# Conv blocks 1 to 3 stay in SBUF and their layernorm is held in code order; two more scheduling conditions

## The chip, the cores and the metric

One core of one Trainium2 chip. The time is device microseconds (us) of one execution, the median of three runs: 2671.15 before the change (2670.78 to 2677.89).

## What is computed

One encoder layer over 2048 tokens of width 1024 in float32, with 256 memory tokens (`rmsnorm`, `layernorm` and the projections are the usual ones):

```python
y = rmsnorm(h, norm_mix_g) @ w_in                      # q, k, v of 8 heads; a, g of the conv branch
att = dilated_sliding_attention(q, k, v)               # windows 128, 512, 2048 at dilations 1, 4, 16
u = a * sigmoid(g)
u = depthwise_conv(u, width 31, 512 channels) + conv_b
conv = silu(layernorm(u, conv_ln_g, conv_ln_b))        # mean and variance over the 512 channels
h = h + concatenate([att, conv]) @ w_out
h = h + cross_attention(rmsnorm(h), rmsnorm(mem)) @ w_xo
h = h + square(relu(rmsnorm(h) @ w_up)) @ w_down
return rmsnorm(h, norm_final_g)
```

The three dilated attentions of a head are joined by a softmax over their log-denominators.

## The kernel before

Tokens are split into four blocks of 512 (p = 0 to 3). Activations lie transposed, channels on the 128 partitions and 512 tokens along a row, so the 512 conv channels are four tiles of 128x512 (c = 0 to 3). Matrix products are done as three fp16 matmuls (`mm3`, L374 to L376), of high and low halves; `split_to` makes the two halves of a weight tile, the high one on ACT (L361) and the low one on DVE (L362).

For each block, `post(p)` does the out projection (`o`, weights `ws_o`), cross attention (`x`, `s`), and the MLP (`up`, `dn`). While `post(p)` runs, the attention of block p+1 and the convolution of block p+1 are woven into it as side generators; for p = 1 and 2 the weight combinations of the MLP (`pw`, `ps`, `pt`) are a third side. The convolution of "pass n" (block n) therefore runs inside `post(n-1)`: its layernorm lies near 1000 to 1090 us for pass 1, 1580 to 1660 for pass 2, 2110 to 2200 for pass 3. Pass 0's is part of the first stage and its layernorm runs beside the first attention.

- `conv_unit` (L391): for each c, 31 multiply-adds on DVE from `cu` into `cacc`, and a store of `cacc` to DRAM (`cscr`).
- `conv_ln` (L411 to L456): loads the four tiles back as `lc`; sums them on DVE (L414, L415, L416); column sums by PE against ones (`lps..m`, L411); a broadcast back by PE (`lrb`, L355), subtraction (L424), squares on ACT (L425, L427), `lps..v`, a Newton rsqrt on DVE (L348 to L350), a second broadcast (`lrc`), the product on DVE (L439, four of them); silu on ACT (L442, four, ahead of them a table load), and the split of the result into `lhl` (ACT L450, DVE L451), stored to `cath` and `catl`.
- `combine` (L1164 to L1202): joins the three attentions of a head pair; L1164 is its first step on DVE, a minimum over `ld`, which a DMA loads from `oscr`.
- In the MLP of blocks 1 and 2, `quad` forms products by a scheme with seven or eight block products, named B11, T1, T32, T4 and so on; its copies (ACT L1656), sums (DVE L1660), relu (L1662), squares (ACT L1664) and splits (L1632, L1633) free PSUM for the next product.
- `norm` in `post` (L1801 ff.): the rms sum of the MLP's input, PE `nps` (L1468), DVE rsqrt, PE `nrb` (L355), ACT copy into `rsb`. For p < 2 it runs in two steps, one behind each of the first two up tiles.

The order on each engine is decided by a scheduler that simulates a timeline. The code influences it by `after(stack, names)`: instructions issued inside may not be put ahead of the last instruction noted under these names ("pe", "dve", "act": `last[...]`, noted at some lines). `pinned(gen, names)` does that for every step of a generator. Pools give each tag a number of buffers.

Of the kernel before, what the change touches and what calls it, by code (L numbers as in the profile page):

```python
# [10 lines left out]
F32 = mybir.dt.float32  # L11
# [4 lines left out]
AF = mybir.ActivationFunctionType  # L16
ALU = mybir.AluOpType
# [4 lines left out]
P = 128  # L22
# [26 lines left out]
def hybrid_layer(ctx, tc, A, out):  # L49
# [7 lines left out]
    def dma(o, i, q=None):  # L57
        return (q or nc.sync).dma_start(o, i)
# [18 lines left out]
    last = {}  # L77
# [6 lines left out]
    def pinned(gen, *names):  # L84

        while True:
            with ExitStack() as st:
                after(st, *names)
                if next(gen, st) is st:
                    return  # L90
            yield
# [267 lines left out]

    def split_to(t, raw, scale):  # L360
        ACT.activation(t[:, 0], raw, AF.Copy, scale=scale)  # L361
        DVE.scalar_tensor_tensor(t[:, 1], raw, scale, t[:, 0], op0=ALU.mult, op1=ALU.subtract)  # L362
        return t

    def two(t):
# [18 lines left out]
        dma(u, uscr[c][:, 512 * n:512 * n + 542])  # L384
        return u

    def conv_unit(c, n, alloc, u):
        acc = alloc("acc", (P, 512), f"cacc{c}_{n}")
        DVE.tensor_scalar(acc, u[:, 0:512], cw[:, c, 0:1], gain("conv_b", c), op0=ALU.mult, op1=ALU.add)
        for t in range(1, CW):  # L390
            DVE.scalar_tensor_tensor(acc, u[:, t:t + 512], cw[:, c, t:t + 1], acc, op0=ALU.mult, op1=ALU.add)  # L391
            if t % 4 == 0:
                yield
        dma(cscr[c][:, 512 * n:512 * (n + 1)], acc)
        yield

    def conv_ln(n, alloc):
        sl = slice(512 * n, 512 * (n + 1))
        cs = []
        for c in range(4):  # L400
            t = alloc(f"cs{c}", F32, f"lc{n}_{c}")
            dma(t, cscr[c][:, sl])
            cs.append(t)
# [520 lines left out]
    def ln_tiles(pl):  # L924
        def alloc(role, dtype, name, shape=(P, 512)):
            if role[:3] == "col":
                return pl.tile(list(shape), F32, tag="cl_" + role, name=name)
            if role[:2] == "cs":
                return pl.tile(list(shape), F32, tag="u" if role[2] < "2" else "acc", name=name, bufs=2)
            return pl.tile(list(shape), dtype, tag="vr", name=name, bufs=2)  # L930
        return alloc

    def conv_units(pl, n, cs=(0, 1, 2, 3), ahead=True):
        def alloc(role, shape, name):
            return pl.tile(list(shape), F32, tag=role, name=name, bufs=2)

        u = conv_load(cs[0], n, alloc)
        yield
        yield
        for i, c in enumerate(cs):  # L940
            nxt = conv_load(cs[i + 1], n, alloc) if ahead and i + 1 < len(cs) else None
            yield from conv_unit(c, n, alloc, u)
            u = nxt or (conv_load(cs[i + 1], n, alloc) if i + 1 < len(cs) else None)

    def conv(pl, n):

        yield from pinned(conv_units(pl, n), "dve")
        yield from conv_ln(n, ln_tiles(pl))

    def both(*gens):  # L950
        for _ in zip(*gens):
# [193 lines left out]
    def combine(p, pr, o0):  # L1145
# [14 lines left out]
        mm_ = sm_[:, 0].rearrange("p (j h) -> p j h", h=2)  # L1160
        W = DVE if end or p > 1 else POOL
        with ExitStack() as st:
            after(st, "dve")
            DVE.tensor_tensor(mm_, ld[:, 0, :, :, HD + 1], ld[:, 1, :, :, HD + 1], op=ALU.min)  # L1164
            DVE.tensor_tensor(mm_, mm_, o0[:, :, :, HD + 1], op=ALU.min)
        W.tensor_tensor(e3[:, 0], mm_, o0[:, :, :, HD + 1], op=ALU.subtract)
# [526 lines left out]
    def post(p):  # L1693
# [104 lines left out]

        def norm(step, st={}):

            if step == 0:  # L1801
                st[0] = rstd_from(ssum)
            elif step == 1:
                rb = ps("c", "nrb")
                bcast_rows(rb, st[0], 4)
                ACT.activation(rsb, rb, AF.Copy, scale=K_UP)

        held = None if p > 1 else []
        if held is None:
# [344 lines left out]
```

## Time and profile before

| what | value |
|---|---|
| runs | 2677.89, 2670.78, 2671.15 us |
| profiled execution | 2675.08 us |
| its span, first to last instruction | 2673.3 us |
| mean granted TensorE clock | 0.993 |
| PE, DVE, ACT, POOL busy | 97%, 73%, 46%, 8% |

Times in the profile count from the span's start. A timeline row has the start, the duration, the engine and line, the operation with its output and inputs, a count, and in brackets the idle time ahead of it on that engine and what ended it.

### The profile page before, as it was taken

The page shows a single profiled execution, that of the slowest core. Times are in us where ns is not written, and L with a number is a line of the kernel's source. Part 1 is how long each engine was busy: PE and PEld are TensorE (multiplying, and loading weights), DVE is VectorE, ACT ScalarE, POOL GpSimd, SP SyncE. Part 2 cuts the span into 40 slices and gives each one's busy share as a digit, 9 for nine tenths or more (in the row PEclk, how much of TensorE's full clock was granted, in tenths as well). Part 3 has the DMA queues.
Part 4 walks back from the last instruction along what each step waited for, and adds up shares of the span by engine and source line. Part 5 has one row for each costly group of instructions (what it writes and reads, how often), then busy time and mean ns, then how long its engine had stood idle before and what let it go on. Part 6 is the DMA issues. An engine that isn't in the chain of part 4 may idle for free. (4 is left out here: it accounts for less than half of the span.)

```text
span 2673.3 us, 45710 instructions
## 1 busy us (share of the span) xinstructions
PE 2602.2 (97%) x17782; PEld 1660.2 (62%) x17782; DVE 1942.8 (73%) x3751; ACT 1236.1 (46%) x2182; POOL 226.4 (8%) x285
## 2 busy tenths in 40 slices
PE   8999999999899999999999999999999999999998
PEld 7844448766454455445576676555776674468876
DVE  5886656577679996556699985467999856676566
ACT  5737545476455344434553343255443434453223
POOL 1234102132002011000000000000000000000000
PEclk9999999999999999999999999999999999999999
DMA  9977968665626777865357677454787775345442
GB/s 268 296 258 219 285 225 264 184 193 170 171 84 172 232 223 213 269 189 171 105 164 221 217 226 232 143 169 123 221 267 242 243 245 159 100 136 163 156 139 80
DMA packets 447048, 523.66 MB, mean 196 GB/s; under 512 B 89997, under 2 KB 341825, under 8 KB 446064
## 3 DMA queue, kind: packets, MB, share of 16 engines
q1 hardware_dynamic: 439424, 505.73, 61.8%
q10 hardware_dynamic: 5184, 9.01, 0.9%
q0 software_dynamic: 2224, 6.01, 0.6%
q8 instruction: 139, 2.28, 0.4%
q14 instruction: 77, 0.63, 0.1%
HBM read 389.18 MB, written 131.48 MB: 195 GB/s over the span
## 5 line engine op out<-in xcount | busy, mean ns | idle before, releaser
L391 DVE SCALAR_TENSOR_TENSOR cacc<-cu,cw,cacc 128x512 f32<-128x512 f32 x480 | 364.4, 764 | 5.0
L375 PE MATMUL dn<-hhl,ws_d 128*128 128x512 f16 x768 | 291.5, 380 | 0.8 <-DVE hhl L1633 0.5
L376 PE MATMUL dn<-hhh,ws_d 128*128 128x512 f16 x768 | 291.5, 380 | 0.0
L374 PE MATMUL dn<-hhh,ws_d 128*128 128x512 f16 x768 | 289.0, 380 | 1.7 <-ACT hhh L1632 1.0
L1024 ACT ACTIVATE sm<-sm,o 128x256 f32<-128x256 f32 (+1 forms) x288 | 119.4, 455 | 129.2 <-DVE o L1023 128.9
L1023 DVE CUSTOM_DVE_ANT_0 sm<-s,mask,qks 128x256 f32<-128x256 f32 (+1 forms) x384 | 151.3, 432 | 32.1 <-PE s L1064 31.2
L1034 DVE TENSOR_TENSOR pl<-pt,ph 128x512 f16<-128x512 f32 x160 | 109.4, 684 | 41.6 <-ACT ph L1033 40.9
L376 PEld LDWEIGHTS <-ws_d 128*128 128x128 f16 x768 | 75.3, 98 | 90.5 <-issue 1.8
L1878 DVE SCALAR_TENSOR_TENSOR h<-dn,bd,h 128x512 f32<-128x512 f32 x96 | 71.6, 748 | 78.9 <-PE dn L376 76.9
L1033 ACT CAST ph<-pt 128x512 f16<-128x512 f32 x160 | 91.4, 572 | 79.6 <-PE pt L1030 79.5
L375 PEld LDWEIGHTS <-ws_d 128*128 128x128 f16 x768 | 75.2, 98 | 83.6 <-issue 1.2
L374 PEld LDWEIGHTS <-ws_d 128*128 128x128 f16 x768 | 75.3, 98 | 83.4 <-issue 1.5
L375 PEld LDWEIGHTS <-ws_t 128*128 128x128 f16 x1064 | 104.3, 98 | 23.2 <-issue 9.5
L374 PEld LDWEIGHTS <-ws_t 128*128 128x128 f16 x1064 | 104.5, 98 | 15.0
L376 PEld LDWEIGHTS <-ws_t 128*128 128x128 f16 x1064 | 104.4, 98 | 14.1
L1030 PE MATMUL pt<-ident,sm 128*128 128x128 f32 x640 | 98.8, 276 | 9.0 <-DVE catl L1202 4.1
L376 PE MATMUL o<-cath,ws_o 128*128 128x512 f16 x256 | 97.3, 383 | 4.6 <-DVE ws_o L362 4.6
L1030 PEld LDWEIGHTS pt<-ident,sm 128*128 128x128 f32 x640 | 78.7, 142 | 34.5 <-ACT sm L1024 4.1
L374 PE MATMUL o<-cath,ws_o 128*128 128x512 f16 x256 | 97.3, 382 | 0.8 <-ACT cath L1201 0.7
L374 PE MATMUL x<-pth,ws_b 128*128 128x512 f16 x256 | 95.7, 379 | 2.3 <-ACT pth L1742 1.2
L375 PE MATMUL o<-catl,ws_o 128*128 128x512 f16 x256 | 97.8, 382 | 0.0
L375 PE MATMUL up<-ml,ws_u 128*128 128x512 f16 x256 | 97.5, 381 | 0.3 <-DVE ml L1512 0.3
(548 smaller groups left out, 7707.4 us busy)
## 6 DMA issues: line engine op xcount, KB each, us to landing
ws_t<-ust SPq DMA_DIRECT2D x133, 512.0 KB
ws_d<-wst SPq DMA_DIRECT2D x80, 512.0 KB
ust<-pt SPq DMA_DIRECT2D x48, 512.0 KB
scan<-in_w_up_dram SPq DMA_DIRECT2D x32, 512.0 KB
scan<-in_w_down_dram SPq DMA_DIRECT2D x32, 512.0 KB
raw_o<-in_w_out_dram SPq DMA_DIRECT2D x32, 512.0 KB
raw_a<-ascr SPq DMA_DIRECT2D x32, 512.0 KB
raw_b<-bscr SPq DMA_DIRECT2D x32, 512.0 KB
```

The lines of the kernel that those rows point to most:

```text
L374: PE.matmul(o, lh, rh, start=first, stop=False, skip_group_check=more)
L375: PE.matmul(o, lh, rl, start=False, stop=False, skip_group_check=more)
L376: last["pe"] = PE.matmul(o, ll, rh, start=False, stop=end, skip_group_check=more)
L391: DVE.scalar_tensor_tensor(acc, u[:, t:t + 512], cw[:, c, t:t + 1], acc, op0=ALU.mult, op1=ALU.add)
L1023: last["dve"] = DVE.tensor_tensor_reduce(dst, so, mask[:, 256 * m:256 * m + nk], SCORE, 3e38, ALU.add, ALU.min, mn)
L1024: last["act"] = ACT.activation(dst, dst, AF.Exp, bias=mn, scale=-1.0)
L1030: last["pe"] = PE.transpose(pt[:, j, :], sm[:, j, :], ident)
L1033: ACT.copy(ph, pt)
L1034: DVE.tensor_tensor(pl, pt, ph, op=ALU.subtract)
L1878: last["dve"] = DVE.scalar_tensor_tensor(hs[m], pt, K_DN, hs[m], op0=ALU.mult, op1=ALU.add)
```

## The change

Three edits. First, the conv passes 1 to 3 keep their four `cacc` tiles in SBUF (tags `cs0` to `cs3`, one buffer each) and hand them to `conv_ln`, which no longer stores and loads them; `conv_ln`'s own tiles (sum, q, hi) now share the tag `u` with the conv inputs, in two buffers. Every step of `conv_ln` is pinned behind the last noted instruction of PE, ACT and DVE. Second, `norm` for p < 2 is put behind the last noted PE matmul. Third, the last combination of block 0 (head pair 3) has its first two steps put behind the last weight split as well, which `split_to` now notes. Pass 0's conv still goes through DRAM.

```diff
--- before.py
+++ after.py
@@ -359,7 +359,7 @@
 
     def split_to(t, raw, scale):
         ACT.activation(t[:, 0], raw, AF.Copy, scale=scale)
-        DVE.scalar_tensor_tensor(t[:, 1], raw, scale, t[:, 0], op0=ALU.mult, op1=ALU.subtract)
+        last["split"] = DVE.scalar_tensor_tensor(t[:, 1], raw, scale, t[:, 0], op0=ALU.mult, op1=ALU.subtract)
         return t
 
     def two(t):
@@ -384,20 +384,24 @@
         dma(u, uscr[c][:, 512 * n:512 * n + 542])
         return u
 
-    def conv_unit(c, n, alloc, u):
-        acc = alloc("acc", (P, 512), f"cacc{c}_{n}")
+    def conv_unit(c, n, alloc, u, kept=None):
+        acc = alloc("acc" if kept is None else f"cs{c}", (P, 512), f"cacc{c}_{n}")
         DVE.tensor_scalar(acc, u[:, 0:512], cw[:, c, 0:1], gain("conv_b", c), op0=ALU.mult, op1=ALU.add)
         for t in range(1, CW):
             DVE.scalar_tensor_tensor(acc, u[:, t:t + 512], cw[:, c, t:t + 1], acc, op0=ALU.mult, op1=ALU.add)
             if t % 4 == 0:
                 yield
-        dma(cscr[c][:, 512 * n:512 * (n + 1)], acc)
-        yield
-
-    def conv_ln(n, alloc):
+        if kept is None:
+            dma(cscr[c][:, 512 * n:512 * (n + 1)], acc)
+        else:
+            kept.append(acc)
+        yield
+
+    def conv_ln(n, alloc, cs=None):
         sl = slice(512 * n, 512 * (n + 1))
-        cs = []
-        for c in range(4):
+        load = cs is None
+        cs = cs or []
+        for c in range(4 if load else 0):
             t = alloc(f"cs{c}", F32, f"lc{n}_{c}")
             dma(t, cscr[c][:, sl])
             cs.append(t)
@@ -925,27 +929,26 @@
         def alloc(role, dtype, name, shape=(P, 512)):
             if role[:3] == "col":
                 return pl.tile(list(shape), F32, tag="cl_" + role, name=name)
-            if role[:2] == "cs":
-                return pl.tile(list(shape), F32, tag="u" if role[2] < "2" else "acc", name=name, bufs=2)
-            return pl.tile(list(shape), dtype, tag="vr", name=name, bufs=2)
+            return pl.tile(list(shape), dtype, tag="u", name=name, bufs=2)
         return alloc
 
-    def conv_units(pl, n, cs=(0, 1, 2, 3), ahead=True):
+    def conv_units(pl, n, cs=(0, 1, 2, 3), ahead=True, kept=None):
         def alloc(role, shape, name):
-            return pl.tile(list(shape), F32, tag=role, name=name, bufs=2)
+            return pl.tile(list(shape), F32, tag=role, name=name, bufs=1 if role[:2] == "cs" else 2)
 
         u = conv_load(cs[0], n, alloc)
         yield
         yield
         for i, c in enumerate(cs):
             nxt = conv_load(cs[i + 1], n, alloc) if ahead and i + 1 < len(cs) else None
-            yield from conv_unit(c, n, alloc, u)
+            yield from conv_unit(c, n, alloc, u, kept)
             u = nxt or (conv_load(cs[i + 1], n, alloc) if i + 1 < len(cs) else None)
 
     def conv(pl, n):
 
-        yield from pinned(conv_units(pl, n), "dve")
-        yield from conv_ln(n, ln_tiles(pl))
+        cs = []
+        yield from pinned(conv_units(pl, n, kept=cs), "dve")
+        yield from pinned(conv_ln(n, ln_tiles(pl), cs), "pe", "act", "dve")
 
     def both(*gens):
         for _ in zip(*gens):
@@ -1160,7 +1163,7 @@
         mm_ = sm_[:, 0].rearrange("p (j h) -> p j h", h=2)
         W = DVE if end or p > 1 else POOL
         with ExitStack() as st:
-            after(st, "dve")
+            after(st, "dve", *(("split",) if end else ()))
             DVE.tensor_tensor(mm_, ld[:, 0, :, :, HD + 1], ld[:, 1, :, :, HD + 1], op=ALU.min)
             DVE.tensor_tensor(mm_, mm_, o0[:, :, :, HD + 1], op=ALU.min)
         W.tensor_tensor(e3[:, 0], mm_, o0[:, :, :, HD + 1], op=ALU.subtract)
@@ -1798,12 +1801,14 @@
 
         def norm(step, st={}):
 
-            if step == 0:
-                st[0] = rstd_from(ssum)
-            elif step == 1:
-                rb = ps("c", "nrb")
-                bcast_rows(rb, st[0], 4)
-                ACT.activation(rsb, rb, AF.Copy, scale=K_UP)
+            with ExitStack() as es:
+                after(es, *(("pe",) if p < 2 else ()))
+                if step == 0:
+                    st[0] = rstd_from(ssum)
+                elif step == 1:
+                    rb = ps("c", "nrb")
+                    bcast_rows(rb, st[0], 4)
+                    ACT.activation(rsb, rb, AF.Copy, scale=K_UP)
 
         held = None if p > 1 else []
         if held is None:
```

In the changed kernel line numbers are higher by 3 to 5 in the lines named here (L1164 becomes L1167, L362 stays, L414 becomes L418, L1656 becomes L1659). Each engine has as many instructions as before, except that SP issues 24 DMAs fewer.

DVE, in block 0 ahead of the first out projection (`o_03` is the last attention output of block 0, `ws_o` the out projection's weights, `csm` and `ce` the combination's). Before:

```order
L1023 ISA o_03_7839 128x1
L1164 TENSOR_TENSOR csm_8753<-ld_8514 128x8
L1272 COPY o_03_7839<-opt 128x4x65
L1165 TENSOR_TENSOR csm_8753<-csm_8753,o_03_7839 128x8
L362 SCALAR_TENSOR_TENSOR ws_o_8570<-raw_o_8568,bd,ws_o_8570 128x1024
L1166 TENSOR_TENSOR ce_8754<-csm_8753,o_03_7839 128x8
L1167 TENSOR_TENSOR ce_8754<-csm_8753,ld_8514 128x16
L1023 ISA sm,o_10_8826<-s,mask,qks 128x256
L1023 ISA o_10_8826 128x1
L1023 ISA sm,o_10_8826<-s,mask,qks 128x256
L1023 ISA o_10_8826 128x1
L362 SCALAR_TENSOR_TENSOR ws_o_8575<-raw_o_8573,bd,ws_o_8575 128x1024
```

After:

```order
L1026 ISA o_03_7839 128x1
L1275 COPY o_03_7839<-opt 128x4x65
L362 SCALAR_TENSOR_TENSOR ws_o_8570<-raw_o_8568,bd,ws_o_8570 128x1024
L1026 ISA sm,o_10_8826<-s,mask,qks 128x256
L1026 ISA o_10_8826 128x1
L1026 ISA sm,o_10_8826<-s,mask,qks 128x256
L1026 ISA o_10_8826 128x1
L362 SCALAR_TENSOR_TENSOR ws_o_8575<-raw_o_8573,bd,ws_o_8575 128x1024
L1167 TENSOR_TENSOR csm_8753<-ld_8514 128x8
L1037 TENSOR_TENSOR pl<-pt,ph 128x512
L1168 TENSOR_TENSOR csm_8753<-csm_8753,o_03_7839 128x8
L1169 TENSOR_TENSOR ce_8754<-csm_8753,o_03_7839 128x8
```

The first step of the combination (L1164, now L1167) stood ahead of the copy and of two splits of `ws_o`, and now stands behind them and ahead of a step of the attention (L1037).

DVE, at the end of pass 2's convolution (`cacc_2`), where its layernorm starts with three sums. Before:

```order
L1272 COPY o_23_17122<-opt 128x4x65
L1034 TENSOR_TENSOR pl<-pt,ph 128x512
L1191 TENSOR_TENSOR cat_17689<-cat_17689,ld_17075 128x512
L414 TENSOR_TENSOR lsum_17703<-lc_0_17695,lc_1_17697 128x512
L1191 TENSOR_TENSOR cat_17689<-cat_17689,ld_17075 128x512
L1660 TENSOR_TENSOR e_17663<-e_17663,up 128x512
L415 TENSOR_TENSOR lsum_17703<-lsum_17703,lc_2_17699 128x512
L1662 SCALAR_TENSOR_TENSOR e_17663<-e_17663,ssumx_14430 128x512
L1660 TENSOR_TENSOR e_17744<-e_17744,up 128x512
L1023 ISA sm,low_23_17123<-s,mask,qks 128x256
L1023 ISA low_23_17123 128x1
L416 TENSOR_TENSOR lsum_17703<-lsum_17703,lc_3_17701 128x512
```

After:

```order
L418 TENSOR_TENSOR lsum_17679<-cacc_2_14972,cacc_2_15744 128x512
L1550 TENSOR_TENSOR ps_30_17689<-pw_30_17585 128x512
L391 SCALAR_TENSOR_TENSOR cacc_2_16995<-cu_2_16327,cw,cacc_2_16995 128x512
L1185 RECIPROCAL csm_17338<-csm_17338 128x8
L419 TENSOR_TENSOR lsum_17679<-lsum_17679,cacc_2_16329 128x512
L1551 TENSOR_TENSOR pw_30_17585<-pw_30_17584,pw_30_17585 128x512
L1636 TENSOR_TENSOR hhl_5_17513<-e_17545,hhh_5_17512 128x2x256
L391 SCALAR_TENSOR_TENSOR cacc_2_16995<-cu_2_16327,cw,cacc_2_16995 128x512
L1187 TENSOR_TENSOR ce_17339<-ce_17339,csm_17338 128x24
L1275 COPY o_23_17107<-opt 128x4x65
L420 TENSOR_TENSOR lsum_17679<-lsum_17679,cacc_2_16995 128x512
```

The sums (L414 to L416, now L418 to L420) read the loaded `lc` tiles and stood behind the last conv pass, the combination and a copy; now they read the kept tiles, the first two stand between the last conv passes, and the third stands three rows behind the last one.

ACT, at the silu of the same layernorm (`e` is a copy of an up product, `hhh` its split). Before:

```order
L1270 COPY o_23_17122<-opt 128x4x65
L58 DMA oscr_1_89<-o_23_17122 128x528
L442 ACT_TABLE_LOAD
L442 ACTIVATE lc_0_17695<-lc_0_17695,gv 128x512
L442 ACTIVATE lc_1_17697<-lc_1_17697,gv 128x512
L450 ACTIVATE lhl_18303<-lc_0_17695,bd 128x512
L442 ACTIVATE lc_2_17699<-lc_2_17699,gv 128x512
L442 ACTIVATE lc_3_17701<-lc_3_17701,gv 128x512
L1656 COPY e_18267<-up 128x512
L450 ACTIVATE lc_0_17695<-lc_1_17697,bd 128x512
L450 ACTIVATE lc_1_17697<-lc_2_17699,bd 128x512
L1664 ACTIVATE e_18267<-e_18267 128x512
```

After:

```order
L1273 COPY o_23_17107<-opt 128x4x65
L58 DMA oscr_1_89<-o_23_17107 128x528
L1659 COPY e_18243<-up 128x512
L446 ACT_TABLE_LOAD
L446 ACTIVATE cacc_2_14972<-cacc_2_14972,gv 128x512
L446 ACTIVATE cacc_2_15744<-cacc_2_15744,gv 128x512
L446 ACTIVATE cacc_2_16329<-cacc_2_16329,gv 128x512
L446 ACTIVATE cacc_2_16995<-cacc_2_16995,gv 128x512
L454 ACTIVATE lhl_18279<-cacc_2_14972,bd 128x512
L1667 ACTIVATE e_18243<-e_18243 128x512
L1027 ACT_TABLE_LOAD
L1027 ACTIVATE sm<-sm,o_30_19193 128x256
```

The first copy (L1656, now L1659) stood behind the table load and four silus and now stands ahead of them; the four silus come in one piece, and the second copy of an up product is behind them, a split, the square and L1027.

On PE the rows of `nps` and `nrb` stand at the same places among the up matmuls in both kernels.

## The prediction

> **What bounds the kernel now.** I read the page's engine table first, then PE's list of waits, then a table of busy time by stage, and last the timelines of the three stages that stood out. The page's head and first row:
>
> ```profile
> span 2673.3 us, 45710 instructions
> ...
> PE 2602.2 (97%) x17782; PEld 1660.2 (62%) x17782; DVE 1942.8 (73%) x3751; ACT 1236.1 (46%) x2182; POOL 226.4 (8%) x285
> ```
>
> PE works 97% of the span, so at most 71 us can come from taking away its waits, and nothing that runs beside PE counts unless PE waits for it. PE's waits, by what it waited for (total in us, times, longest):
>
> ```profile
> PE up L374 <- ACT e L1656: 6.8, 2, 5.4
> PE o L376 <- DVE ws_o L362: 4.6, 1, 4.6
> ...
> PE nrb L355 <- DVE nr L350: 2.8, 1, 2.8
> ...
> PE lps2m L411 <- DVE lsum L416: 2.3, 1, 2.3
> ```
>
> These four are long single waits, and each belongs to a line near the change: the out projection's weight split, the silu part of a conv norm, the norm's rsqrt and a conv norm's sums. The table by stage (start:end, length, PE busy, then the other engines, the granted TensorE clock, DMA share, GB/s) shows how much they weigh:
>
> ```profile
> 560.00:700.00 140.00, 126.96 (x1290) 89.08 (x1287) 93.46 (x355) 83.88 (x207) 32.35 (x57) 0.98 0.62 177
> ...
> 1000.00:1090.00 90.00, 89.27 (x528) 46.84 (x527) 60.55 (x106) 48.19 (x71) 12.42 (x14) 1.00 0.75 224
> ...
> 1580.00:1660.00 80.00, 72.25 (x476) 45.08 (x474) 46.81 (x91) 30.56 (x50) 1.89 (x2) 0.94 0.71 219
> ...
> 2110.00:2200.00 90.00, 89.88 (x620) 59.72 (x620) 55.07 (x96) 33.62 (x52) 1.01 (x1) 1.00 0.73 246
> ```
>
> The stretch 1580 to 1660 is the conv norm of pass 2 and its silu. It has 7.75 us of idle PE, and a clock of 0.94: PE is not only idle there, it also runs slower for a while afterwards. Pass 3 has the same work at 2110 to 2200 and 0.12 us of idle PE, and pass 1 (1000 to 1090) has 0.73, so in these two the change can only keep the time or lose some.
>
> **The change part by part.** The DVE work of the convolution is not touched: the same 480 passes stay.
>
> ```profile
> L391 DVE SCALAR_TENSOR_TENSOR cacc<-cu,cw,cacc 128x512 f32<-128x512 f32 x480 | 364.4, 764 | 5.0
> ```
>
> Kept tiles remove 24 transfers (12 stores, 12 loads, 256 KB each, 6.3 MB of 523.66 MB). With DMA shares of 0.6 to 0.75 in these stages I count nothing for the bytes themselves; what counts is the wait for their landing.
>
> Place A, the first out projection (pass 0). DVE, then ACT, then PE:
>
> ```profile
> 681.25 0.08 DVE L1023 DVE_READ_ACCUMULATOR2_ANT o<- 128x1 f32 x1
> 685.16 0.17 DVE L1164 TENSOR_TENSOR csm<-ld 128x8 f32<-128x8 f32 x1 [3.83 <-issue]
> 685.25 0.42 DVE L1272 COPY o<-opt 128x260 f32<-128x260 f32 x1
> ...
> 685.67 1.28 DVE L362 SCALAR_TENSOR_TENSOR ws_o<-raw_o,bd,ws_o 128x1024 f16<-128x1024 f32 x1
> ```
> ```profile
> 678.37 2.17 ACT L361 ACTIVATE ws_o<-raw_o,bd 128x1024 f16<-128x1024 f32 x2
> ```
> ```profile
> 687.01 0.61 PE L376 MATMUL o<-cath,ws_o 128*128 128x512 f16 x1 [4.59 <-DVE ws_o L362]
> ```
>
> DVE is free at 681.3 and stands at L1164, which reads the tile that a load of oscr fills; behind it wait the copy L1272 and the split L362, whose ACT half ended at 680.5. In the new order L1164 stands behind two splits. Then the copy runs at 681.3 (0.42) and the split at 681.7 (1.28), and it ends at 683.0 at the latest. PE, which waits from 682.42, waits 0.6 instead of 4.59: 4.0 us. The wait has a second price, as the clock column (after the four engines and POOL) of the stretch behind it shows:
>
> ```profile
> 687.01:691.95 4.94, 4.94 (x14) 2.26 (x15) 2.82 (x9) 1.13 (x3) 0.00 (x0) 0.50 1.00 310
> ```
>
> 4.94 us of PE work at half clock would be 2.47 at full clock: 2.5 us more. A gives 6.5. What is late next: L1164 now stands ahead of L1034 (its pl feeds the attention output), but the load that it waits for lands by 685.2, before that step is reached. If that cover fails, a wait of about 2 us comes back, A's lower bound is 4.5.
>
> Place D, the sums of pass 2's conv norm. DVE, then PE, then the clock behind it:
>
> ```profile
> 1576.54 0.74 DVE L391 SCALAR_TENSOR_TENSOR cacc<-cu,cw,cacc 128x512 f32<-128x512 f32 x1
> ...
> 1583.73 0.69 DVE L414 TENSOR_TENSOR lsum<-lc,lc 128x512 f32<-128x512 f32 x1 [2.41 <-DMA lc<-cscr]
> ...
> 1587.75 0.69 DVE L416 TENSOR_TENSOR lsum<-lsum,lc 128x512 f32<-128x512 f32 x1
> ```
> ```profile
> 1588.49 1.05 PE L411 MATMUL lps2m<-ones,lsum 128*128 128x1 f32 x8 [2.31 <-DVE lsum L416]
> ```
> ```profile
> 1589.65:1593.07 3.42, 3.42 (x10) 1.27 (x9) 3.42 (x8) 2.39 (x4) 0.00 (x0) 0.52 0.64 254
> ```
>
> The last conv pass ends at 1577.3, but L414 starts at 1583.7, since the tile goes to DRAM and back. With the tiles kept, L414 and L415 (0.69 each) run between the last conv passes and L416 follows two instructions behind the last one, so it ends near 1580, before PE gets there (it was free at 1586.18). The wait of 2.31 goes, and with it 3.42 us at 0.52, worth 1.6: D gives 3.9. Bounds: 2.3 if the clock drops anyway for another gap; above 3.9 I see nothing.
>
> The Trainium skill, "TensorE: Matmul & The Clock Gate", in its table of Part 1 ("What's actually happening"), lets the clock fall to half after at least one idle window of about 3.4 us. By that rule a gap of 2.31 us costs no clock and D would be 2.3; the row above has 0.52 right behind such a gap, so here the measurement decides and D stays.
>
> Place E, silu and output of pass 2. DVE, PE with its clock, then ACT:
>
> ```profile
> 1646.23 0.17 DVE L1164 TENSOR_TENSOR csm<-ld 128x8 f32<-128x8 f32 x1 [6.54 <-DMA ld<-oscr]
> 1646.32 2.47 DVE L439 TENSOR_TENSOR lc<-lc,lrc 128x512 f32<-128x512 f32 x4
> ```
> ```profile
> 1645.27 0.27 PE L1064 MATMUL s<-k,qh 128*128 128x256 f16 x1
> 1645.38 0.27 PE L1064 MATMUL s<-k,ql 128*128 128x256 f16 x1
> 1651.10 0.37 PE L374 MATMUL up<-T32h,ws_t 128*128 128x256 f16 x1 [5.45 <-ACT e L1656]
> ```
> ```profile
> 1647.70:1654.50 6.80, 3.40 (x17) 2.34 (x17) 5.62 (x14) 5.96 (x10) 0.00 (x0) 0.51 0.30 111
> ```
> ```profile
> 1647.04 1.52 ACT L442 ACTIVATE lc<-lc,gv 128x512 f32<-128x512 f32 x2 [13.17 <-DVE lc L439]
> ...
> 1650.48 0.56 ACT L1656 COPY e<-up 128x512 f32<-128x512 f32 x1
> ...
> 1653.12 0.61 ACT L1664 ACTIVATE e<-e 128x512 f32<-128x512 f32 x1
> 1653.75 1.28 ACT L1024 ACT_TABLE_LOAD   x1
> 1655.04 0.51 ACT L1024 ACTIVATE sm<-sm,o 128x256 f32<-128x256 f32 x1
> 1655.46 0.60 ACT L1632 CAST hhh<-e 128x512 f16<-128x512 f32 x1
> ```
>
> ACT stood 13 us before its first silu, since DVE stood at L1164 with the four L439 behind it, and the copy e of the up product, which frees PE, stood behind four silus. In the new order the first copy stands ahead of the table load, so PE's T32 product follows at 1645.6: the wait of 5.45 and the slow stretch (3.40 us of work at 0.51, so 1.7) go, 7.1 together. But DVE's order there is unchanged: the sum L1660 comes behind L1164, four L439 (to 1648.8) and three small ones of L1164's kind, and ends near 1649.8. PE has T32 (24 matmuls of 128x256, with 0.11 between starts as in the two scores above) done at 1648.2 and then wants the buffer that this sum reads: a new wait of 1.7. Next it wants the second copy, which on ACT is behind four silus (from 1647.0, 3.0 in all), a split, L1664, the table load, L1024 and L1632: some 1654.1, where PE is at 1652.5: a new wait of 1.5. So E gives 7.1 - 1.7 - 1.5 = 3.9. Ends: 7.1 if the load of L1164 lands earlier and both waits vanish; 0.5 if PE's clock falls for two windows like the one above (6.80 us at 0.51, 3.4 lost). I take 3.9, as the rows after which these waits end are all there.
>
> Place F, the same norm in pass 3:
>
> ```profile
> 2148.72 2.48 DVE L439 TENSOR_TENSOR lc<-lc,lrc 128x512 f32<-128x512 f32 x4 [2.84 <-PE lrc L355]
> ```
> ```profile
> 2148.88 1.28 ACT L442 ACT_TABLE_LOAD   x1
> ...
> 2159.20 0.59 ACT L1656 COPY e<-up 128x512 f32<-128x512 f32 x1
> ```
>
> Now ACT does L1664, L1632 and two more copies ahead of the table load. From L439's end (2151.2) that is two DVE sums of 0.69, 0.61, 0.60, two copies of 0.56, 1.28, the silus at 0.76 each and one split: the fourth copy comes at 2159.5 to 2160.1 instead of 2159.2. I count 0.5 lost, between 0 and 3 (a wait of D's size with a slow stretch). In pass 1 the L414 to L416 come a few instructions later and its silus one tile later; PE waits 0.73 there now, and I count nothing, at worst the same 3.
>
> The norm sums: the added condition moves no row. The sums and the transposes of nrb keep their places on PE among the up matmuls, so nrb's wait of 2.8, and the slow stretch that follows it, stay. Zero; if rows moved at run time after all it could give the 2.8 and what this window lost (5.80 us of work at 0.51, so 2.8):
>
> ```profile
> 855.80:862.60 6.80, 5.80 (x31) 3.15 (x30) 6.80 (x16) 4.42 (x10) 2.32 (x3) 0.51 0.82 202
> ```
>
> **Sum.** 6.5 + 3.9 + 3.9 - 0.5 = 13.8 us. The profiled execution took 2675.08, its span 2673.3 and 1.8 around it, and lies 3.9 over the median of the runs, 2671.15. 2675.1 - 13.8 = 2661.3 for the profiled one, and 2657.3 against the median. Forecast: 2657.3, its own range about 2655 to 2663, as far as the losses in A, D, E and F add up in part. A measurement here tells some 0.3% from no change, so the border is 2663.1.
>
> **Rivals.** First: the waits only move. At E both new waits come and the clock falls for two windows (0.5), F loses 3, D keeps 2.3: 2671.2 - 6.5 - 2.3 - 0.5 + 3 = 2665, within 0.3%. For it speaks that DVE's order at E is unchanged and that a gap of 2.31 us was enough for half clock; against it that two gaps of 1.7 and 1.5 are each smaller. The skill's rule named above would give those gaps no clock loss; this kernel's window behind D makes that unsure.
>
> Second, slower: the conv norm, now held in the order of the code on PE, ACT and DVE, makes PE stand at the sums and the broadcasts of passes 1, 2 and 3. Six such stops of D's size (2.3 and 1.6) are 23.4; with A's 6.5 kept and D's and E's gains gone into them: 2671.2 - 6.5 + 23.4 = 2688. From four stops on (2680) it is slower than before by over 0.3%. Against it: in pass 2 the sums end near 1580, six us before PE was free for them, and in pass 3 PE has other matmuls in its row between those of the norm.
>
> Third, better: the two new waits at E vanish (7.1 instead of 3.9), or the norm's wait or slow stretch goes (up to 5.6): 2657.3 - 3.2 to 2657.3 - 5.6, so 2654 to 2652, and 2649 with both. For it: the slow stretches above last 3.42 us or twice that, so they seem to come in fixed windows, and all work behind A stands 6.5 us elsewhere in them; against it, the norm's 2.8 us wait has its rows where they were.
>
> Fourth: the change doesn't do what it says. For the norm sums this is so by the order. For the whole it would need L1164 to stay ahead of the split, and it doesn't: 2671.
>
> **How the numbers follow.** Forecast 0.55, first rival 0.17, second 0.07, third 0.15, fourth 0.06. Faster by over 0.3%: forecast, third, and a quarter of the first (0.04), 0.74. Within: the rest of the first and the fourth, 0.19. Slower: the second, 0.07. The range takes in the third and the first rival: 2649 to 2667; outside are the second, the fourth and what my bounds miss.
>
> **What would show it.** A: on PE the wait of L376 for the split at 682 under 1 us, and no row of 0.63 for a 128x512 matmul behind it. D: no wait of lps2m, L414 before the last conv pass. E: T32 follows the scores at once, then waits of one to two us for DVE's sum and ACT's copy; their absence is the third rival, a clock of 0.5 behind them the first. F: PE busy all but 0.1 to 1 us of those 90. The norm: a wait of 2.8 for nrb, as now. Wrong would be a new PE wait of over 2 us in pass 1 or 3, or L1164 holding L1034 at A.

## The result, and the profile after

The changed kernel took 2661.11 us (median of 6 runs, 2660.24 to 2663.99), the kernel before 2673.44 (6 runs, 2670.5 to 2677.89). The ratio is 0.9955, with an interval of 0.9942 to 0.9968: 12.0 us less, 0.45%. Forecast were 13.8 us less and 2657.3, in a range of 2649 to 2667. The profiled execution took 2661.2 us.

The page's head, PE's row of the engines, and PE's list of waits, of the changed kernel:

```profile
span 2659.4 us, 45676 instructions
...
PE 2599.7 (98%) x17782; PEld 1660.0 (62%) x17782; DVE 1940.9 (73%) x3751; ACT 1235.7 (46%) x2182; POOL 227.4 (9%) x285
```
```profile
PE nrb L355 <- DVE nr L350: 2.8, 1, 2.8
...
PE up L374 <- ACT e L1659: 1.2, 1, 1.2
...
PE o L376 <- DVE ws_o L362: 0.4, 1, 0.4
```

Of the four long waits, three are nearly gone: the split at A went from 4.6 to 0.4, ACT's copy at E from 5.4 to 1.2 (the 6.8 of the list before has a second wait in it, of 1.3 at 1993), and the wait for lps2m (2.3) is not in the list any more. The norm's 2.8 stands as it was. In the table by stage, the clock shows the second part of the gain (its column is the third from the end):

```profile
500.00:560.00 60.00, 55.90 (x637) 47.77 (x636) 45.71 (x180) 46.30 (x111) 15.18 (x16) 0.97 0.51 156
560.00:700.00 140.00, 132.56 (x1352) 92.97 (x1351) 98.65 (x367) 86.58 (x214) 33.41 (x58) 1.00 0.63 182
...
1580.00:1660.00 80.00, 78.55 (x566) 52.48 (x565) 51.34 (x101) 36.15 (x61) 1.90 (x2) 1.00 0.77 238
...
2110.00:2200.00 90.00, 90.00 (x607) 58.51 (x605) 51.31 (x88) 35.03 (x55) 1.01 (x1) 1.00 0.66 216
```

PE idles 1.45 us between 1580 and 1660, where it idled 7.75, and the clock is 1.00 there and in the stage of A, where it was 0.94 and 0.98. But between 500 and 560, where no row has moved, the clock is now 0.97 where it was 1.00: a slow stretch that the profiled execution of before did not have. So two executions cannot be compared by their spans alone.

I therefore matched the PE instructions of each trace with those of before and took the difference of their starts at places ahead of and behind each stage. The table has the change of that difference from one place to the next, in us (negative: the stage got shorter); the places are the starts 541, 679, 701, 1570, 1595, 1635, 1700, 2077 and 2215 or next to them in the trace of before. For instance, the o matmul at 679.35 before starts at 682.38 after (+3.03) and one at 701.47 starts at 698.25 (-3.22), so A is worth -6.2. The other kernels are told of below.

| kernel | start to A | A | A to D | D | E | E to F | F | whole span |
|---|---|---|---|---|---|---|---|---|
| changed | +3.0 | -6.2 | -1.5 | -4.2 | -4.9 | -1.3 | +1.2 | -13.9 |
| changed, once more | +0.3 | -6.4 | -0.8 | -4.2 | -5.0 | -0.9 | +1.6 | -15.5 |
| last combination alone | +5.0 | -5.8 | -0.9 | -2.1 | -0.2 | -1.4 | +1.6 | -3.7 |
| pin alone | -0.1 | +0.7 | -0.2 | -2.8 | -4.8 | -1.2 | +0.5 | -8.0 |
| kept alone | +0.3 | -0.5 | -0.2 | -4.2 | 0.0 | -1.4 | -0.2 | -6.2 |
| kept and pin | +0.2 | -0.7 | -1.8 | -4.2 | -4.9 | +0.8 | +1.3 | -9.4 |
| stores put back | +0.2 | -6.6 | -1.2 | -4.2 | -5.1 | -0.8 | +1.9 | -16.1 |
| E's remaining wait | -0.3 | -5.9 | -1.5 | -4.2 | -5.5 | -0.6 | +2.9 | -15.1 |
| last layernorm free | +1.8 | -5.8 | -1.4 | -4.2 | -4.8 | -0.3 | -0.2 | -14.8 |

The columns A and E are nearly the same in every kernel that has the part and near zero in the others. D is different, as the next section shows: half or more of what D gave in the profile comes without the kept tiles. F is told of under the last layernorm. The columns "start to A" and "E to F" belong to no part: up to A no row has moved in any of them, and the gain from E to F comes in nearly every kernel, since before's execution had a wait there that the others have shorter or not at all:

```profile
1993.02 0.27 PE L374 MATMUL up<-T32h,ws_t 128*128 128x256 f16 x1 [1.33 <-ACT e L1656]
```

### The profile page after: what moved, and what is told of

The parts are those of the page before. It is cut to its first block, busy times and chain, and to the rows that moved or that the text cites. A ratio compares the mean times of both kernels' runs of the same rounds, so it can differ in the third digit from the quotient of the medians.

```text
span 2659.4 us, 45676 instructions
## 1 busy us (share of the span) xinstructions
PE 2599.7 (98%) x17782; PEld 1660.0 (62%) x17782; DVE 1940.9 (73%) x3751; ACT 1235.7 (46%) x2182; POOL 227.4 (9%) x285
## 4 chain that ended last, share of the span: by engine, by line
PE 73%; DVE 13%; DMA 7%; ACT 2%; issue 2%; SPq 1%; POOL 1%; DVEq 0%; POOLq 0%; ACTq 0%
PE dn L375 7%; PE dn L376 7%; PE dn L374 7%; PE up L374 6%; PE up L376 6%; PE up L375 6%; DVE cacc L391 4%; PE lin L376 3%; PE lin L374 3%; PE lin L375 3%; PE xs L375 2%; PE xs L376 2%; PE xs L374 2%; PE x L375 2%; PE pt L1033 2%
## 5 line engine op out<-in xcount | busy, mean ns | idle before, releaser
L1027 ACT ACTIVATE sm<-sm,o 128x256 f32<-128x256 f32 (+1 forms) x288 | 119.7, 455 | 124.7 <-DVE o L1026 124.4
L1037 DVE TENSOR_TENSOR pl<-pt,ph 128x512 f16<-128x512 f32 x160 | 109.4, 684 | 44.8 <-ACT ph L1036 44.0
L374 PE MATMUL up<-mh,ws_u 128*128 128x512 f16 x256 | 97.2, 380 | 0.5 <-ACT mh L1514 0.5
L374 PE MATMUL o<-cath,ws_o 128*128 128x512 f16 x256 | 96.5, 379 | 0.8 <-ACT cath L1204 0.7
L375 PE MATMUL xs<-ws_a,yh 128*128 128x512 f16 x256 | 97.0, 379 | 0.3 <-DVE ws_a L362 0.2
L375 PE MATMUL x<-ptl,ws_b 128*128 128x512 f16 x256 | 97.0, 379 | 0.3 <-DVE ptl L1746 0.3
```

Source lines behind the costliest of these rows:

```text
L374: PE.matmul(o, lh, rh, start=first, stop=False, skip_group_check=more)
L375: PE.matmul(o, lh, rl, start=False, stop=False, skip_group_check=more)
L1027: last["act"] = ACT.activation(dst, dst, AF.Exp, bias=mn, scale=-1.0)
L1037: DVE.tensor_tensor(pl, pt, ph, op=ALU.subtract)
```

## The experiments

The times are medians of 5 to 12 runs beside the kernel before on the same chip. The ratio is that to the kernel before, with its interval in brackets, and a gain in us is taken from the ratio unless two times stand beside it.

**The last combination alone.** The kernel before, with this edit alone:

```diff
-        DVE.scalar_tensor_tensor(t[:, 1], raw, scale, t[:, 0], op0=ALU.mult, op1=ALU.subtract)
+        last["split"] = DVE.scalar_tensor_tensor(t[:, 1], raw, scale, t[:, 0], op0=ALU.mult, op1=ALU.subtract)
...
-            after(st, "dve")
+            after(st, "dve", *(("split",) if end else ()))
```

> Only the condition on the last combination of block 0 (behind the last weight split). Theory (three PE waits, each with its own part of the change): only place A changes; the wait of PE for the split (4.6 us) falls under 1 us, the slow clock behind it goes, the waits of 2.3 (lps2m) and 5.4 (T32) stay; about -6.1 us against before. Rival (the gain is the kept tiles' lighter DMA and SP queue): near 0 here.

Measured: 2665.96, ratio 0.9978 (0.9969 to 0.9986), 5.9 us less. Its PE rows at A, D and E are these:

```profile
687.88 0.39 PE L376 MATMUL o<-cath,ws_o 128*128 128x512 f16 x1 [0.51 <-DVE ws_o L362]
...
1586.39 1.05 PE L411 MATMUL lps2m<-ones,lsum 128*128 128x1 f32 x8 [1.90 <-DVE lsum L416]
...
1647.03 0.37 PE L374 MATMUL up<-T32h,ws_t 128*128 128x256 f16 x1 [5.17 <-ACT e L1656]
```

A gave 5.8 of its 6.2, E nothing. The scheduler also moved 34 rows of DVE between 863 and 896 here, as it did in the changed kernel; the column A to D, which has them, shows -0.9 and -1.5. At D the order is that of before, and yet the stage is 2.1 shorter. The wait is 1.90 instead of 2.31: the first sum starts 6.3 us behind the last conv pass instead of 6.45, and PE comes to the column sums 0.26 us later against that pass. And no slow stretch followed:

```profile
1580.00:1600.00 20.00, 18.10 (x122) 11.24 (x120) 18.36 (x35) 9.95 (x17) 0.50 (x1) 1.00 0.84 246
```

**The pin alone, and the kept tiles alone.** In the first, only `conv_ln` is pinned and the tiles go through DRAM (the edit is to the kernel before); in the second they are kept and `conv_ln` is free (the edit is to the changed kernel, and the conditions of the last combination and of the norm, not shown here, are taken out as well):

```diff
-        yield from conv_ln(n, ln_tiles(pl))
+        yield from pinned(conv_ln(n, ln_tiles(pl)), "pe", "act", "dve")
```

> Only the layernorm's steps held in code order on PE, ACT and DVE; tiles still go through DRAM. Theory: place E alone changes (the first copy ahead of the silus); T32's wait of 5.4 goes, 1.2 to 3.2 us of new waits come; the wait of 2.3 for lps2m stays with its slow clock; -4 to -6 us. Rival (lighter DMA): near 0. Second rival (the pin gives all of the conv's gain): -9.

```diff
-        yield from pinned(conv_ln(n, ln_tiles(pl), cs), "pe", "act", "dve")
+        yield from conv_ln(n, ln_tiles(pl), cs)
```

> Only the tiles kept in SBUF, the layernorm free in order. Theory: place D alone changes; the wait of lps2m goes with its slow clock, T32's wait of 5 us stays; -4 to -5 us. Rival (lighter DMA makes everything behind it earlier): -9 or more, with T32's wait shorter too. Second rival (the pin does it): near 0.

Measured: 2667.18, ratio 0.9985 (0.9977 to 0.9994), 4.0 us less with the pin; 2668.04, 0.9985 (0.9977 to 0.9994), 4.0 less with the tiles (by the medians, 3.2). The pin's rows on PE, at A and D, and then that of the tiles alone at E:

```profile
687.15 0.61 PE L376 MATMUL o<-cath,ws_o 128*128 128x512 f16 x1 [4.87 <-DVE ws_o L362]
...
1587.76 1.05 PE L411 MATMUL lps2m<-ones,lsum 128*128 128x1 f32 x8 [1.22 <-DVE lsum L416]
```
```profile
1646.25 0.37 PE L374 MATMUL up<-T32h,ws_t 128*128 128x256 f16 x1 [5.24 <-ACT e L1659]
```

So E is the pin's work and not the kept tiles': with the pin E gives 4.8, with the tiles alone 0.0 and the wait of over 5 us is still there. D's wait was only 1.22 in the pin's trace, in which no row ahead of it in pass 2 has moved. Of the three executions in which the tiles go through DRAM it was 2.31, 1.90 and 1.22, and only the first was followed by half clock. The kept tiles alone give all of D, but what they are worth depends on the execution with which they are compared: D is 4.2 us shorter than in before's, 2.1 than in that of the last combination alone, and 1.4 than in the pin's.

**Both, without the last combination** (and without the norm's condition).

> Tiles kept and the layernorm pinned, without the condition on the last combination: D and E change, A stays with its wait of 4.6 and half clock. Theory: the parts add up, -9 to -10 us here, and this plus the one with the condition alone gives the whole change. Rival: the parts overlap (a later stage waits for the same thing), then this one is within 3 us of the whole change.

Measured: 2665.66, ratio 0.9978 (0.9969 to 0.9986), 5.9 less where 9 to 10 were expected. A's wait of PE was 4.8, as expected, and the stages D and E gave 4.2 and 4.9 in the trace. The 9.4 of its span were measured against an execution of 2675.08; the median of before in this call is 2671.26, 3.8 lower. Against that it is 5.6, and this agrees. The two halves of the change, 5.9 and 5.9, add up to 11.8, and the whole gave 12.0, so no overlap of the two shows. Each has an interval of some 2.3 us to either side, as have the pin's 4.0 and the tiles' 4.0, whose sum is 8.0 beside 5.9 for both; the times cannot settle that, and the stages of the trace show D and E side by side.

**The norm's condition.** No run has it alone, but the traces show that it moves no row. On PE, DVE and ACT 754, 308 and 120 places in the order differ between the kernel before and the changed one. They are the 742, 257 and 115 of "kept and pin" and the 12, 51 and 5 of "last combination alone", with the same rows in them, and neither of these two kernels has the condition.

**The changed kernel again**, as the yardstick:

> The changed kernel itself once more, as the yardstick for the other three of this call: -12 us against before, within 2 us. In its trace the slow stretches behind A, D and E are gone again; whether one follows the 2 us wait near 546 us differs from execution to execution, since nothing in the order decides it.

Measured: 2659.57, ratio 0.9954 (0.9942 to 0.9967). Its trace is the second row of the table. The slow stretch behind the 2 us wait came here too (a clock of 0.50 from 543.70 to 547.10).

**Traffic put back.** If bytes counted, and not waits, the stores and loads would cost time even when nobody waits for them:

```diff
             kept.append(acc)
+            dma(cscr[c][:, 512 * n:512 * (n + 1)], acc)
+            for e in range(2):
+                dma(alloc("spare", (P, 256), f"sp{c}_{n}{e}"), cscr[c][:, 512 * n + 256 * e:512 * n + 256 * (e + 1)])
...                                                    # the spare tile has one buffer
```

> The changed kernel, with the stores of the conv tiles and loads of them put back (into a spare tile that nobody reads, in halves of 128 KB): the same bytes as before, but nothing waits for them. The rows of PE, DVE, ACT and POOL are the changed kernel's. Theory (the wait for the round trip counted, not the bytes): the same time as the changed kernel within 1 us. Rival (lighter DMA and SP queue): it gives back at least half of what keeping the tiles gave, 2 us or more, and the load ld at E lands later.

Measured: 2667.33, ratio 0.9984 (0.9975 to 0.9992): 8 us of the 12 are lost. That spoke for the rival, but the trace shows another reason. SP's queue, then ACT and PE in this kernel:

```profile
1940.96 0.46 SPq L58 DMA_DIRECT2D cscr<-cacc  x1
1941.47 0.42 SPq L58 DMA_DIRECT2D cu<-uscr  x1
1947.18 0.32 SPq L58 DMA_DIRECT2D sp<-cscr  x1
1947.60 0.38 SPq L58 DMA_DIRECT2D ws_t<-ust  x1
```
```profile
1979.26 1.15 ACT L1535 ACTIVATE pt<-pw,bd 128x1024 f16<-128x1024 f32 x1 [9.13 <-DMA pw<-in_w_up_dram]
```
```profile
1982.11 0.37 PE L374 MATMUL up<-T32h,ws_t 128*128 128x256 f16 x1 [5.03 <-ACT e L1662]
```

My load of a tile stands two rows behind its store, and SP issues nothing for 5.3 us until the store has landed; the second half, which needs the same spare tile, holds it for another 2.8. The weights behind it are late, pw lands late, ACT stands at it for 9.13 us, and PE for 5.03, with a clock of 0.50 in the four us behind. From E to F this trace loses 6.9 us where the changed kernel's gains 1.3, which is the 8. The kernel before had its loads at the end of each pass only; in pass 2 SP's gap ahead of the last of them was 2.2 us (1578.58 to 1580.80). So this run priced longer holds than the change removed. Two more were meant to put the traffic back without them. First the stores alone:

```diff
-        if kept is None:
-            dma(cscr[c][:, 512 * n:512 * (n + 1)], acc)
-        else:
+        dma(cscr[c][:, 512 * n:512 * (n + 1)], acc)
+        if kept is not None:
             kept.append(acc)
```

> The changed kernel with the 12 stores of the conv tiles put back (nobody reads them): half of the bytes that the change removed, without the loads. Rows of PE, DVE, ACT and POOL as in the changed kernel. Theory (waits of the SP queue for a round trip cost, bytes do not): the changed kernel's time, -11 to -13 us against before. Rival (bytes cost): +2 to +4 us against the changed kernel.

Measured: 2663.66 (runs of 2658.99 to 2666.32), ratio 0.9963 (0.995 to 0.9976), 9.9 us less than before where 11 to 13 were expected. That is 2.4 us over the changed kernel by the ratios, which is what the rival said, and 4.1 by the medians; the intervals overlap. Its trace speaks for the theory: A, D and E give 6.6, 4.2 and 5.1, no less than in the changed kernel. But the execution profiled is the fastest of the five. Whether the bytes of the stores cost some 2 to 4 us isn't settled. Then stores and, at the start of each layernorm, four copies from DRAM to DRAM:

```diff
+        for c in range(0 if load else 4):
+            dma(cspare[c][:, sl], cscr[c][:, sl])
```

> As the one before, and four copies from DRAM to DRAM at the start of each layernorm, where the kernel before had its loads: SP waits for the last store as it did before, the bytes are those of before and more, and nothing waits for their arrival. Theory: within 2 us of the changed kernel; what the earlier run with traffic lost (8 us) came from its loads standing behind each single store, which holds SP at 1941.5 to 1947.2 there and makes the ws_t and pw loads late (PE waits 5.0 at 1982). Rival (bytes): again 6 to 8 us lost, with the same wait at 1982.

Measured: 2666.02, ratio 0.9978 (0.9968 to 0.9988), and the wait is back:

```profile
1942.73 0.46 SPq L58 DMA_DIRECT2D cscr<-cacc  x1
1943.24 0.42 SPq L58 DMA_DIRECT2D cu<-uscr  x1
1948.64 0.55 SPq L58 DMA_DIRECT2D cspr<-cscr  x1
```
```profile
1982.32 0.27 PE L375 MATMUL up<-T32h,ws_t 128*128 128x256 f16 x1 [3.63 <-ACT e L1661]
```

The scheduler put each copy close behind its store, although the code has them at the layernorm, and SP was held for 5.0 us again. What I had written for the rival came, 6.4 us lost with the wait at 1982. But most of it is lost where the hold is: from E to F the trace loses 4.6 us, where the changed kernel's gains 1.3. The order was not the one that the run was made for, so it does not tell the hold from the bytes, and what the bytes cost by themselves stays as the run before it left it.

**E's remaining wait.** The changed kernel, with the first step of the last combination of blocks 2 and 3 put behind the norm's product. One row moves on DVE, from ahead of the four L443 at E to behind them:

```diff
-            DVE.tensor_tensor(cs[c], cs[c], rb2, op=ALU.mult)
+            last["ln"] = DVE.tensor_tensor(cs[c], cs[c], rb2, op=ALU.mult)
...
-            after(st, "dve", *(("split",) if end else ()))
+            after(st, "dve", *(("split",) if end else ("ln",) if p > 1 and pr == H // 2 - 1 else ()))
```

> The changed kernel, with the first step of the last combination of blocks 2 and 3 (L1167) behind the conv norm's last product (L443): one DVE row moves, from ahead of the four L443 at E to behind them. Theory: what is left of E's wait (1.2 us for ACT's second copy, 0.25 for DVE's sum) comes from the load that L1167 waits for with the four products behind it. lrc is ready at 1628.5 and DVE free at 1630.7, so the silus start about 1 us earlier; -1.0 to -1.5 us against the changed kernel. Rival (ACT's own work of four silus, table loads and splits sets that wait): 0.

Measured: 2659.35, ratio 0.9953 (0.9939 to 0.9967), the same as the changed kernel's 2659.57; the 1.0 to 1.5 us that were expected would be lost in intervals of this width. PE of the changed kernel (second execution), then of this one:

```profile
1637.79 0.27 PE L374 MATMUL up<-T4h,ws_t 128*128 128x256 f16 x1 [0.93 <-DVE e L1663]
...
1641.99 0.27 PE L374 MATMUL up<-T32h,ws_t 128*128 128x256 f16 x1 [1.20 <-ACT e L1659]
```
```profile
1639.58 0.27 PE L374 MATMUL up<-T32h,ws_t 128*128 128x256 f16 x1 [0.57 <-ACT e L1659]
...
1665.51 0.39 PE L374 MATMUL dn<-hhh,ws_d 128*128 128x512 f16 x1 [1.31 <-DMA ws_d<-wst]
```

The mechanism was right: the two waits fell from 2.13 to 0.57. But 26 us later PE stands 1.31 for a load of ws_d, where the second execution of the changed kernel stood 0.07 and the first 0.95; in the kernel told of next, which has this edit too, it is 2.08. So most of the gain goes to the next wait in line.

**The last layernorm free.** The edit above for block 2 only, and pass 3 without the pin:

```diff
-        yield from pinned(conv_ln(n, ln_tiles(pl), cs), "pe", "act", "dve")
+        ln = conv_ln(n, ln_tiles(pl), cs)
+        yield from pinned(ln, "pe", "act", "dve") if n < 3 else ln
```

> The changed kernel with the last layernorm (pass 3) free in order, and L1167 behind the norm's product for block 2. Theory: the changed kernel's loss at F (1.2 to 1.6 us between 2084 and 2097, PE waits of 1.03 for an up product's sum and 1.11 for a split) comes from pass 3's sums standing ahead of them on DVE in code order; freed, it goes: -1.5 to -2.5 us against the changed kernel, about -14 against before. Rival (the loss comes from keeping the tiles, or from elsewhere): no change, -12.

Measured: 2658.4, ratio 0.9945 (0.9933 to 0.9958), the best of all, 2.4 us under the changed kernel's 0.9954 by the ratios, though the intervals overlap. PE around F in the changed kernel (second execution), then in this one:

```profile
2083.84 0.38 PE L374 MATMUL dn<-hhh,ws_d 128*128 128x512 f16 x1 [1.03 <-DVE e L1663]
...
2094.18 0.38 PE L375 MATMUL dn<-hhl,ws_d 128*128 128x512 f16 x1 [1.11 <-DVE hhl L1636]
```
```profile
2086.18 0.38 PE L374 MATMUL dn<-hhh,ws_d 128*128 128x512 f16 x1 [0.41 <-DVE e L1664]
...
2095.19 0.38 PE L375 MATMUL dn<-hhl,ws_d 128*128 128x512 f16 x1 [0.93 <-DVE hhl L1637]
```

F then costs nothing (-0.2 in the table, where the changed kernel has +1.2 and +1.6). The tiles alone, also with a free layernorm, have -0.2, and kept and pin +1.3, so the loss comes from the pin of the kept tiles' sums; the pin alone, whose sums wait for their loads, has +0.5. Only part of it lies in the two waits shown. The +1.6 of "last combination alone" is something else, since none of its rows at F has moved. Three short gaps of PE stand there close together, and a stretch at half clock follows, worth 1.7:

```profile
2102.47 0.81 PE L374 MATMUL dn<-hhh,ws_d 128*128 128x512 f16 x3 [0.72 <-ACT hhh L1632]
2104.02 0.19 PE L1038 MATMUL opt<-v,ph 128*128 128x65 f16 x1 [0.71 <-ACT o L1270]
2104.71 0.58 PE L375 MATMUL dn<-hhl,ws_d 128*128 128x512 f16 x1 [0.47 <-DVE hhl L1633]
...
2104.70:2108.12 3.42, 3.41 (x9) 1.17 (x9) 2.30 (x4) 0.00 (x0) 0.00 (x0) 0.51 0.99 303
```

The +2.9 of "E's remaining wait" has such a stretch too (0.50 from 2094.10 to 2097.50).

**Gaps by themselves.** What a gap of PE costs beyond its length is a term in A, D and E. This kernel leaves out the whole computation and only makes gaps:

```python
for rep in range(16):
    for g in range(7):
        ...                                            # 80 + 3 * rep matmuls of 128x512 into one bank
        DVE.tensor_scalar(t[:, 0:P], b[:, 0:P], 0.001, None, op0=ALU.mult)
        for _ in range(2 * g):
            DVE.tensor_scalar(t[:, 0:P], t[:, 0:P], 1.0, None, op0=ALU.mult)
        DVE.tensor_scalar(w, t[:, 0:P], 1.0, None, op0=ALU.mult)    # the next burst's weights
```

> Leaves out the whole computation: bursts of 80 to 125 matmuls of 128x512, and between two bursts a gap in which PE waits for DVE steps of 128x128 (2, 4, ... 14 of them, some 0.5 to 3 us), 112 gaps in all. Theory (the clock is decided in fixed windows of about 3.4 us by how idle PE is in one): short gaps never cost clock, gaps near 3 us nearly always, and those between do in some cases, by where they fall in the window. Rival (a threshold in the length of the gap alone, of 3.4 us): no half clock behind any of them.

Two gaps of the same 2.22 us, and the four us behind each, with the clock in the third column from the end:

```profile
82.12 2.45 PE L68 MATMUL b<-r,w 128*128 128x512 f16 x8 [2.22 <-DVE w L73]
```
```profile
227.26 4.92 PE L68 MATMUL b<-r,w 128*128 128x512 f16 x22 [2.22 <-DVE w L73]
```
```profile
82.12:86.12 4.00, 4.00 (x13) 1.56 (x14) 0.00 (x0) 0.00 (x0) 0.00 (x0) 0.65 0.01 4
227.26:231.26 4.00, 4.00 (x19) 1.87 (x20) 0.00 (x0) 0.00 (x0) 0.00 (x0) 1.00 0.00 0
```

For each burst but the first and the last (110 gaps) I took its length less its matmuls at 0.2155 us apart:

| gap, us | 0.65 | 1.17 | 1.70 | 2.22 | 2.74 | 3.26 | 3.79 |
|---|---|---|---|---|---|---|---|
| bursts that lost time | 0 of 16 | 0 of 16 | 0 of 16 | 8 of 16 | 10 of 16 | 10 of 15 | 13 of 15 |

Of the 41 losses 34 are 1.62 to 1.74 us, as 3.4 us at half clock give; the others lie between 1.36 and 3.0. The trace's record of the granted clock has 43 slow stretches, and they all start on one grid of 3.413 us. Folded on it, the starts of the 16 gaps of 2.22 us fall apart cleanly: the 8 with a loss lie within 1.36 us of the period and the other 8 outside. That bears out fixed windows, against a threshold of 3.4 us in the gap alone. Laid on the grid, each of the 41 gaps with a loss puts 2.05 us or more into one window, and each of the other 69 at most 2.01. So here a window with some 2.05 us or more of idle PE makes the next one slow. A gap g from 2.05 on puts so much into one window for 3.41 + g - 2 x 2.05 of 3.41 us of its possible starts: 45, 60, 75 and 91% for the four longer ones, beside 50, 62, 67 and 87% counted, and none for 1.70. In the layer's own traces the border is not sharp: the window ahead of the stretch at 2104.7 shown above has 1.85 us of idle PE by the profile, and in the trace of the stores put back a window with 1.88 (from 843.5 on) is not followed by a slow one, while the next, with 1.69, is. And it is not one gap's length that counts: at 2104.7 three gaps of under 0.8 us were enough.

## Why the prediction was right, point by point

- **A** was forecast at 6.5 and gave 6.2 and 6.4 (5.8 alone). The wait is 0.4 where 0.6 was forecast, and behind it the matmuls run at full clock (1.00 from 684.94 to 689.00). DVE of the changed kernel has L1167 waiting 0.63 for its load, as the step that is late next; L1037 behind it held up nobody:

```profile
684.62 1.28 DVE L362 SCALAR_TENSOR_TENSOR ws_o<-raw_o,bd,ws_o 128x1024 f16<-128x1024 f32 x1
...
688.53 0.17 DVE L1167 TENSOR_TENSOR csm<-ld 128x8 f32<-128x8 f32 x1 [0.63 <-DMA ld<-oscr]
688.62 0.68 DVE L1037 TENSOR_TENSOR pl<-pt,ph 128x512 f16<-128x512 f32 x1
```

- **D** was forecast at 3.9 and gave 4.2 in both traces. The mechanism is the one named: the third sum ends at 1575.3, and its matmul runs at 1580.6 without a wait. But the size was that of one execution: 2.31 of waiting with 1.6 of slow clock is the worst of three, and the others had 1.90 and 1.22 with none. D is worth 1.4 to 4.2, by the execution with the tiles in DRAM with which one compares. This is the term of the sum that was mis-sized; the bound that I set for it from below, 2.3, was too high, and nothing was set for a better one than 3.9.

```profile
1574.64 0.68 DVE L420 TENSOR_TENSOR lsum<-lsum,cacc 128x512 f32<-128x512 f32 x1
```
```profile
1580.57 0.95 PE L415 MATMUL lps2m<-ones,lsum 128*128 128x1 f32 x8
```

- **E** was forecast at 3.9 and gave 4.9 and 5.0. Of the two new waits, ACT's second copy came as forecast (1.20 for 1.5), and DVE's sum took 0.25 and 0.93 instead of 1.7: the load ahead of it took 8.6 us in the changed kernel (issue on SP, first reader on DVE) and 10.8 before (issue on SP, and the reader at 1646.23 shown ahead):

```profile
1627.20 0.37 SPq L58 DMA_DIRECT2D ld<-oscr  x1
```
```profile
1635.80 0.17 DVE L1167 TENSOR_TENSOR csm<-ld 128x8 f32<-128x8 f32 x1 [5.02 <-DMA ld<-oscr]
```
```profile
1635.45 0.37 SPq L58 DMA_DIRECT2D ld<-oscr  x1
```

No clock was lost behind the two waits, as behind none of the probe's gaps up to 1.70.

- **F** was forecast at 0.5 lost and lost 1.2 and 1.6. The place was wrong: the fourth copy, which I watched, made no PE wait; the sums of pass 3 did, more than 50 us earlier on DVE, where they now stand in code order. The times cannot show this loss by itself; the traces of "last layernorm free" and "kept alone" do.

- **The norm** was forecast at zero by the unmoved rows, and its wait is the same 2.8, with a clock of 0.50 from 851.70 to 858.50 behind it.

- **The sum.** 6.2 at A, 1.4 to 4.2 at D, 4.9 at E, less 1.4 at F is 11.1 to 13.9, around the measured 12.0. That the forecast came so near is partly luck: it had 1.0 too little at E, about 0.9 too little lost at F, and up to 2.5 too much at D. And the time forecast was 2657.3 from the median of three runs; six runs put the kernel before at 2673.44, 2.3 higher.

- **The rivals.** That the waits only move came true for some 3 us (1.2 at E, 1.0 and 1.1 at F), without loss of clock in the two traces of the changed kernel; in that of "E's remaining wait" the waits at F were followed by a slow stretch. The slower one did not come: no new wait of over 2 us in passes 1 and 3. Nor did the better one, since both new waits at E, the norm's wait and the slow stretch behind it are there. The Trainium skill's rule ("TensorE: Matmul & The Clock Gate", Part 1) of a whole idle window does not hold here as I read it: half of the gaps of 2.22 us cost a window. But nor was my own reading right, that the row behind a gap of 2.31 us decides it: of the probe's gaps of that size only half lose it.

## What to carry to other kernels

A step that waits for a DMA, put in DVE's order ahead of a step that PE needs, handed its wait on to PE here (3.83 us on DVE, 4.59 on PE); moving one such step behind two weight splits gave half of this gain, and holding the layernorms in code order about a third. Before sizing a wait from one profile, look at whether its length comes from a DMA's landing and whether the slow clock behind it came by chance: take the bound from several executions. Add up the short gaps that stand close together as well. And a load that stood just behind its own store in SP's queue held all issues behind it until the store had landed, here for 5.3 and 5.0 us.

## What was not expected of the hardware

The same gap of 2 to 3.8 us costs clock in one place of the 3.413 us windows and none in another, and so in one execution and not in the next. PE and the clock behind it, before and in the changed kernel, at a place that the change does not touch:

```profile
543.45 0.84 PE L1030 MATMUL pt<-ident,sm 128*128 128x128 f32 x4 [1.98 <-ACT sm L1024]
...
543.45:547.45 4.00, 4.00 (x48) 2.99 (x49) 1.78 (x9) 4.00 (x11) 4.00 (x4) 1.00 1.00 349
```
```profile
546.33 0.84 PE L1033 MATMUL pt<-ident,sm 128*128 128x128 f32 x4 [1.98 <-ACT sm L1027]
...
546.33:550.33 4.00, 4.00 (x31) 2.62 (x32) 1.54 (x9) 3.73 (x10) 4.00 (x4) 0.69 0.99 331
```

A wait of 1.98 us left the clock at 1.00 in the one and was followed by 0.69 in the other. At 1.7 us a time, a few such gaps are a part of the spread of several us between executions of one kernel (2667.01 to 2677.14 in 35 runs of the kernel before); that they are all of it was not shown.
